# A trunk layer's mixers traced in lanes: visits left out behind reciprocal roots, SSD's time steps in a lane of their own, output projection units taken ahead

## The chip, the core and the metric

The kernel runs on one core of a Trainium2 chip: TensorE (PE) for matmuls, VectorE (DVE), ScalarE (ACT) and GpSimd (POOL) beside it, and SyncE (SP) issuing the transfers. Each engine takes its own instructions in the order in which the program holds them and waits on semaphores for the others. The metric is the device time of one execution in microseconds.

## What is computed

One inference step of a two-layer trunk over 128 context tokens and 256 latent tokens (384 rows of width 1024), in float32. Each layer has a token mixer and a squared-ReLU MLP, both between RMS norms with modulation. The mixer projects the rows once, feeds four scan groups of width 256 (RWKV-7, HGRN2, Mamba-2 SSD, RG-LRU, each forward and backward), concatenates them and projects back:

```python
p = modulated(rms_norm(x, g_pre1), shift, scale) @ w_in
out = concat(rwkv7_mix(...), hgrn2_mix(...), ssd_mix(...), rglru_mix(...))   # each forward + backward
x = x + gate * rms_norm(out @ w_out, g_post1)
# inside ssd_mix, for each direction:
dt = softplus(dtr + dt_bias);  acum = cumsum(dt * a_neg)      # the time steps, 4 heads a direction
# inside rwkv7_mix, after both directions:
y = (y - mean) * rsqrt(var + eps) * ln_w + ln_b               # per head, then bonus and gate
```

## The kernel before

Weights are split into two float32r halves (`unit`: one transfer of 512 KB, a copy on ACT, a difference on DVE), and a projection of 384 rows is 24 matmuls into a `pj` bank. 29 column tiles of `w_in` are projected (`projections`, `ORDER`), each copied to a `st` buffer of the stash; at most seven wait there.

The mixers of a layer are written as Python generators, *lanes*, and `mixers` interleaves them while it traces the program. One pass of its `while` loop is a *round*. In a round every lane gets at most one *visit*: it runs up to its next `yield`. A lane that yielded 0 is visited in the first turn of the next round, one that yielded 1 in the second; one that yielded a condition is visited once the condition holds. After the visits the round is filled with projection steps of four matmuls (`supply`) until some 3 us of estimated TensorE time (`ROUND`) have gone by since its start; where no side lane was seen, six steps are put in in any case. The matmuls are held in exactly this order on PE (`T.ordered`). A program that orders instructions by their data places the other engines' work and the transfers.

The lanes: `t0` to `t3` (`rwkv_thread`) run RWKV's twelve chunk groups (pair, direction, group), each a chain of some 18 visits of small matmuls; `rwkv` prepares their inputs (`rwkv_inputs`, `rwkv_vectors`) and finishes pair 0 as a whole and pair 1 group by group (`rwkv_output`); `hg0` and `hg1` are HGRN2's pairs; `right` joins them (`hgrn_end`) and then does `ssd`; `lru` starts when the last projection is made and has fourteen visits, of which the third to the sixth issue its matmuls. When `hg0`, `hg1`, `right` and `lru` are all done, the lane `tail` is added behind the others: the output projection, one unit of `w_out` after the other, 18 matmuls a unit (three visits), from then on three visits a round. HGRN2's units come first, then SSD's and LRU's, then RWKV's first; RWKV's second comes last, 128 rows at a time.

Four places compute 1/sqrt by `rsqrt` (L284 to L303), a row of twelve or so small DVE operations, and use it on PE one visit later: `channel_rms` (HGRN2's and SSD's norms), `rwkv_inputs` (L1300), `rwkv_output` (L1333, then `flips`, a transposition on PE by matmuls). `ssd` begins with the time steps: a transposition of the `lora` tile, a softplus of some twenty small DVE operations (L716 to L729), the products `dta` (L919, L921), and three sums over tokens on PE in the next visit. All of this lies behind `hgrn_end` in the lane `right`.

Of the kernel before, what the change touches and what calls it, by code (L numbers as in the profile page):

```python
# [20 lines left out]
NCTX, NLAT, NT = 128, 256, 384  # L21
# [10 lines left out]
RIGHT = ("hgrn", "ssd", "lru")  # L32
# [34 lines left out]
NTILE = len(COLS)  # L67
GROUPS = ("rwkv", "hgrn", "ssd", "lru")
# [176 lines left out]
class Trunk:  # L245
# [437 lines left out]
    def layer(self, l, h):  # L683
        a = self.a
        self.l = l
        self.lora = None
        pool = lambda nm, side="left": self.tc.tile_pool(name=f"{nm}{l}", bufs=1, side=side, reuse_waits="tile")
        with pool("mo") as self.mo:
            h = self.mixers(l, h)
        with pool("ff") as fp, pool("kf", "right") as kf, ExitStack() as more:  # L690
            mf, half = more.enter_context(pool("mf", "right")), more.enter_context(ExitStack())
            beside = self.modulations(BESIDE[l], half.enter_context(pool("mg", "right")), 8)
            sums = (step for k, v in SUMS[l] for step in self.modulation_sums(k, v, self.mods[k], mf))
            tags = ("r0", "r1"), ("r2", "h"), ("h", "md")
            finish = self.mlp(l, h, fp, HELD, kf, tags, beside, half, sums)
            then = None
            if l + 1 < L:
                self.prepare(a["win"][l + 1, n] for n in ORDER[:FRESH])
                self.l, n = l + 1, self.mods[l + 1]
                then = n["sh1"], n["sc1"]  # L700
            with self.residual(self.mods[l]["g2"], then, range(3), bufs=2) as (step, h):
                for t in range(3):
                    step(t, finish(t), tags[t])
        return h
# [178 lines left out]
    def channel_rms(self, vs, sqt):  # L883

        T = self.T
        sqs = [self.mt([128, NT], sqt[hf]) for hf in range(2)]
        for hf in range(2):
            self.S.activation(sqs[hf], vs[hf], AF.Square)
        yield 1
        ss = self.bank()  # L890
        for i in range(3):
            for hf in range(2):
                T.matmul(ss[:, i:i + 1], sqs[hf][:, i * 128:i * 128 + 128], self.onec, start=hf == 0, stop=hf == 1)
        m = self.small(3, "crm")
        self.V.tensor_scalar(m, ss[:, 0:3], 1.0 / 256, EPS, op0=OP.mult, op1=OP.add)
        r = self.rsqrt(m, 3, "cr")
        yield 1
        bc = self.bank()
        for i in range(3):
            T.transpose(bc[:, i * 128:i * 128 + 128], r[:, i:i + 1].to_broadcast([128, 128]), self.c("ident"))  # L900
        return bc


    def ssd(self, l):
        V, S, T = self.V, self.S, self.T
        lt = yield from self.lora_tile()
        s0 = self.state("s_ss", [2, 256])
        yield 1
        tp = self.bank()
        for i in range(3):  # L910
# [9 lines left out]
                     self.aneg[l][:, None, 0:4].to_broadcast([128, 3, 4]))  # L920
        V.tensor_mul(an.rearrange("p (i d h) -> p d i h", i=3, d=2)[:, 1], dt[:, 1],  # L921
                     self.aneg[l][:, None, 4:8].to_broadcast([128, 3, 4]))
        yield 1
        cps = self.bank()
        T.matmul(cps[:, 0:12], self.c("le"), a3[:, :, 0:4], start=True, stop=True)
        T.matmul(cps[:, 12:24], self.c("ge"), a3[:, :, 4:8], start=True, stop=True)
# [12 lines left out]
            V.tensor_mul(w4[:, d], w4[:, d], dt[:, d])  # L939
        S.activation(ea, ac, AF.Exp)  # L940
        S.activation(et, et, AF.Exp)

        xbc = []
        for n in range(6):
            acc = self.mt([128, GAP], f"sx{n}")
# [326 lines left out]
    def rwkv_inputs(self, p):  # L1272
# [25 lines left out]
        r = self.rsqrt(m, 6, "rk")  # L1298
        rx = self.mt([128, NT], "rb", 3).rearrange("p (h e) -> p h e", h=6)
        V.tensor_copy(rx, r[:, :, None].to_broadcast([128, 6, 64]))  # L1300
        yield 1
        ps = self.bank()
        for i in range(3):
            T.transpose(ps[:, i * 128:i * 128 + 128], rx[:, 2 * i:2 * i + 2, :].rearrange("p h e -> p (h e)"), ident)
# [13 lines left out]
    def rwkv_output(self, p, lora, bonus, ytok, out, g=None):  # L1318
# [12 lines left out]
        V.tensor_scalar(vr, vr, 1.0 / 64, GN_EPS, op0=OP.mult, op1=OP.add)  # L1331
        r = self.rsqrt(vr, n, "rk")
        V.tensor_mul(y, y, r[:, :, None].to_broadcast([128, n, 64]))  # L1333
        yield 0
        ps = self.bank()
        for i in range(n):
            self.flips(ps[:, i * 64:i * 64 + 64], y[:, i, :])
# [183 lines left out]
    def mixers(self, l, h):  # L1521
# [2 lines left out]

        self.outs, self.made, self.turns, self.taken = {}, {}, [], set()
        self.scans, self.scanned, self.left = {}, set(), {}
        self.groups = [(p, d, g) for p in range(2) for d in range(2) for g in ((0, 2, 1) if d else (0, 1, 2))]
# [8 lines left out]
        with pool("st", "left") as self.stash, pool("rwkv", "left") as rwkv, ExitStack() as early:  # L1538
# [3 lines left out]

            flow = {"proj": self.projections(l, h), "mods": self.modulations(EARLY[l], self.ahead, FRESH)}
            lanes = {"t0": self.rwkv_thread(0), "t1": self.rwkv_thread(1), "t2": self.rwkv_thread(2), "t3": self.rwkv_thread(3),
                     "rwkv": self.rwkv(l),
                     "hg0": self.hgrn(l, 0), "hg1": self.hgrn(l, 1), "right": right(), "lru": self.lru(l)}
            self.lanes, side = lanes, {"hg0", "hg1", "right", "lru"}
            room, kind, waits = dict.fromkeys(lanes, rwkv), dict.fromkeys(lanes, 0), {}
# [28 lines left out]
                self.moded = self.moded or f == "mods" and n < most  # L1577
                return n
            supply("proj", self.T.ns + 1e9, FIRST * 24 // PSTEP)
            n, tail, made = 0, None, 0  # L1580
            while lanes:
                n += 1
                begin = self.T.ns
# [9 lines left out]
                if tail is None:  # L1593
                    if n * MODS > made and not self.moded:
                        made += supply("mods", 1e18, 1)
                    got = supply("proj", begin + ROUND)
                    if not side & seen:
                        got += supply("proj", begin + 1e9, URGENT // PSTEP - got)
                    assert seen or got, (l, n, list(lanes))
                else:  # L1600
                    while "tail" in lanes and (self.T.ns < begin + ROUND or len(lanes) == 1) and visit("tail"):
                        pass
        return self.normed

    def tail(self, l):

# [5 lines left out]
        def split(v, n):  # L1612
# [3 lines left out]
            self.S.activation(hi, v, AF.Copy)  # L1616
            self.V.tensor_sub(lo, v, hi.bitcast(F32))
            return hi, lo
        for i, k in enumerate([2 * GROUPS.index(k) + j for k in RIGHT for j in range(2)] + [0]):
            if k == 0:  # L1620
                yield from self.need("p0")
            w = self.unit(a["wout"][l, k])
            x = split(self.outs[GROUPS[k // 2]][:, k % 2, :], NT)
            for t in tiles:
                self.tokens_by_cols(acc[t], w, x, t, i == 0, False)
                yield 1
        self.prepare(a["w1"][l, n] for n in range(FRESH))

# [33 lines left out]
```

## Time and profile before

| | |
|---|---|
| median of 3 runs | 1466.03 us (1465.28 to 1476.91) |
| the profiled execution | 1468.26 us, span 1466.5 us |
| mean granted TensorE clock | 0.94 |
| mixers, layer 0 and layer 1 | about 98 to 440 us and 765 to 1157 us |
| MLPs, layer 0 and layer 1 | the stretches behind them, to 764 us and to the end |
| HBM traffic over the span | 127 GB/s |

The page gives the busy time of each engine over the span; the waits say which instruction an engine stood still for, and whose result it was; the timeline gives instructions in order of time, with the idle time ahead of one in brackets; the windows give the same busy times for stretches. A granted clock of 1.00 is 2.4 GHz, 0.50 is 1.2 GHz; a mean between them is a mixture.

### The profile page before, as it was taken

How to read it: one execution, taken by the hardware profiler on the slowest of the kernel's cores; microseconds unless marked ns; L12 is line 12 of the kernel's file. 1: busy time of each engine (PE TensorE's matmuls, PEld its weight loads, DVE VectorE, ACT ScalarE, POOL GpSimd, SP SyncE). 2: the span in 40 equal slices, each digit the busy share in tenths (PEclk: the TensorE clock that was granted, in tenths of full speed). 3: DMA queues.
4: the chain of work that ended last, by engine and by line, in shares of the span. 5: the costliest groups of instructions: out<-in, count | busy, mean ns of one | idle time of the engine just before them, and what ended most of it. 6: DMA issues, size and time to landing. Idle time of an engine off the chain costs nothing.

```text
span 1466.5 us, 29196 instructions
## 1 busy us (share of the span) xinstructions
PE 1310.9 (89%) x12128; PEld 1134.5 (77%) x12128; DVE 920.4 (63%) x2155; ACT 578.8 (39%) x1028; POOL 49.9 (3%) x100
## 2 busy tenths in 40 slices
PE   6899997997587989999989999798965789999997
PEld 2678886886366788899869899687854679889986
DVE  4587467956747878395374767766675585424534
ACT  4453224432724332244254533443245434324423
POOL 0002020000001000000010012000000000000000
PEclk9899997998788999999999999999985999999999
DMA  9544331111256867463451111111120463433333
GB/s 336 169 151 149 114 99 55 59 60 55 87 187 197 297 217 234 143 224 131 154 196 62 59 44 56 61 48 47 46 103 10 153 202 118 160 130 129 124 128 122
DMA packets 56321, 187.59 MB, mean 128 GB/s; under 512 B 6492, under 2 KB 9580, under 8 KB 55164
## 3 DMA queue, kind: packets, MB, share of 16 engines
q1 hardware_dynamic: 56188, 185.73, 37.8%
q8 instruction: 95, 1.56, 0.5%
q14 instruction: 38, 0.31, 0.1%
HBM read 178.28 MB, written 7.43 MB: 127 GB/s over the span
## 4 chain that ended last, share of the span: by engine, by line
PE 66%; DVE 19%; DMA 7%; ACT 5%; issue 2%; SPq 0%; POOL 0%; DVEq 0%; ACTq 0%
PE pj L239 31%; PE r L239 17%; PE h L239 12%; PE md L239 5%; DVE wl L614 3%; DMA w<-in_mod_w_dram 2%; DVE ma L492 2%; ACT wh L613 2%; DMA ms<-in_mod_w_dram 2%; DMA gp<-in_norm_g_dram 1%; DMA raw<-in_wout_dram 1%; ACT junk L535 1%; DVE sx L782 1%; DVE rP L1407 1%; DVE x L604 1%
## 5 line engine op out<-in xcount | busy, mean ns | idle before, releaser
L614 DVE TENSOR_TENSOR wl<-raw,wh 128x1024 fp32r<-128x1024 f32 x202 | 247.3, 1224 | 264.9 <-ACT wh L613 262.2
L613 ACT ACTIVATE wh<-raw 128x1024 fp32r<-128x1024 f32 x202 | 213.9, 1059 | 383.2 <-PE md L239 154.6
L239 PE MATMUL pj<-hhi,wl 128*128 128x384 f32 (+2 forms) x1024 | 350.2, 342 | 8.0 <-DVE wl L614 8.0
L239 PE MATMUL pj<-hlo,wh 128*128 128x384 f32 (+2 forms) x1024 | 349.4, 341 | 5.1 <-DVE hlo L567 4.6
L239 PE MATMUL pj<-hhi,wh 128*128 128x384 f32 (+2 forms) x1024 | 351.0, 343 | 2.2 <-ACT relu L626 2.0
L239 PEld LDWEIGHTS pj<-hhi,wh 128*128 128x128 f32 x1024 | 198.8, 194 | 16.3 <-issue 8.2
L239 PEld LDWEIGHTS pj<-hlo,wh 128*128 128x128 f32 x1024 | 198.8, 194 | 12.9 <-issue 5.4
L239 PEld LDWEIGHTS pj<-hhi,wl 128*128 128x128 f32 x1024 | 199.0, 194 | 12.6 <-DVE wl L614 9.6
L492 DVE SCALAR_TENSOR_TENSOR ma<-ms,csil,ma 128x1024 f32<-128x1024 f32 x70 | 86.9, 1277 | 4.0 <-DMA ms<-in_mod_w_dram 4.0
L627 DVE TENSOR_TENSOR relu<-relu 128x384 f32<-128x384 f32 x64 | 35.2, 551 | 1.0 <-ACT relu L626 1.0
L626 ACT ACTIVATE relu<-pj 128x384 f32<-128x384 f32 x64 | 30.3, 474 | 13.2 <-PE pj L239 13.2
L239 PE MATMUL pj<-w,csil 128*32 128x512 f32 x64 | 21.5, 725 | 12.5 <-DMA w<-in_mod_w_dram 12.5
L239 PE MATMUL r<-rI,rW 64*64 64x64 f32 x528 | 31.9, 222 | 0.0
L1434 DVE TENSOR_TENSOR rI<-rI,r 128x256 f32<-128x256 f32 (+1 forms) x66 | 25.0, 392 | 9.9 <-PE r L239 9.3
L1129 ACT ACTIVATE hk<-hK 128x384 f32<-128x384 f32 x24 | 13.5, 564 | 42.3 <-PE r L239 28.4
L239 PE MATMUL r<-rI,rP 64*64 64x64 f32 x480 | 23.4, 223 | 6.8 <-DVE rI L1416 5.1
L239 PEld LDWEIGHTS r<-rI,rW 64*64 64x64 f32 x528 | 24.9, 134 | 5.0 <-issue 3.4
L579 POOL TENSOR_TENSOR xs<-x,scale 128x512 f32<-128x512 f32 x9 | 12.6, 1397 | 469.0 <-DVE x L604 253.6
L239 PEld LDWEIGHTS r<-rI,rP 64*64 64x64 f32 x480 | 18.2, 134 | 12.9 <-issue 5.3
L239 PE MATMUL r<-rW,rI 64*64 64x64 f32 x432 | 27.0, 218 | 0.0
L239 PE MATMUL pj<-wh,o 128*128 128x512 f32 x64 | 22.8, 441 | 3.5 <-ACT wh L613 3.5
L1434 DVE TENSOR_TENSOR rI<-rI,h 128x256 f32<-128x256 f32 (+1 forms) x45 | 17.0, 383 | 12.5 <-PE h L239 11.9
(951 smaller groups left out, 2619.7 us busy)
## 6 DMA issues: line engine op xcount, KB each, us to landing
raw<-in_w_dram SPq DMA_DIRECT2D x128, 512.0 KB
raw<-in_win_dram SPq DMA_DIRECT2D x58, 512.0 KB
mw<-in_mod_w_dram SPq DMA_DIRECT2D x40, 512.0 KB
ms<-in_mod_w_dram SPq DMA_DIRECT2D x40, 512.0 KB
w<-in_mod_w_dram SPq DMA_DIRECT2D x16, 512.0 KB
raw<-in_wout_dram SPq DMA_DIRECT2D x16, 512.0 KB
xd<-x SPq DMA_DIRECT2D x9, 512.0 KB
x<-xd SPq DMA_DIRECT2D x9, 512.0 KB
```

The source lines that it names most:

```text
L239: return self.put(self.engine.matmul(out, left, right, **k), left, right)
L492: V.scalar_tensor_tensor(acc[:, r, :], w, c, acc[:, r, :], op0=OP.mult, op1=OP.add)
L535: self.S.activation(junk, v, AF.Square, scale=1.0 / 32, accum_out=acc[:, i:i + 1])
L604: self.V.scalar_tensor_tensor(v, ys[n], r, v, op0=OP.mult, op1=OP.add)
L613: self.S.activation(hi, v, AF.Copy)
L614: self.V.tensor_sub(lo, v, hi.bitcast(F32))
L626: self.S.activation(r, ps[:, :NT], AF.Relu)
L627: self.V.tensor_mul(r, r, r)
L782: self.V.scalar_tensor_tensor(out, x[:, j:j + GAP], w[j], out, op0=OP.mult, op1=OP.add)
L1129: S.activation(k.rearrange("p (b i t) -> p b i t", i=2, t=h), sides(K, h), AF.Copy)
L1407: V.tensor_mul(prod.rearrange("p u j i t -> p (u j) (i t)"), ps.rearrange("p (q m) -> p q m", q=4), mask[:, None, :].to_broadcast([128, 4, ...
L1434: V.tensor_sub(flat[:, f], flat[:, f], ps[:, 128 if h == 32 else 0:256].rearrange("p (q s) -> p q s", s=64))
```

## The change

The diff is shown but for its empty lines and unchanged neighbours. `rest(n, kind)` yields n + 1 times, so a lane issues nothing for n visits. It stands for one visit in `channel_rms` and in `rwkv_inputs` ahead of the transpositions, and for two visits in `rwkv_output` ahead of the flips. SSD's time steps become a lane `steps` that starts when the `lora` tile is there, in the first round of the mixers, with two visits left out between `dta` and the sums; `ssd` waits for their results. In the first round after the last projection that projects nothing, the first two units of the output projection are requested. In `tail`, the inputs of two units are split ahead of the first unit, and then one unit ahead.

```diff
 # channel_rms, behind r = self.rsqrt(m, 3, "cr")
-        yield 1
+        yield from self.rest(1, 1)
+    def rest(self, n, kind):
+        for _ in range(n + 1):
+            yield kind
-    def ssd(self, l):
+    def ssd_steps(self, l):
         V, S, T = self.V, self.S, self.T
-        lt = yield from self.lora_tile()
-        s0 = self.state("s_ss", [2, 256])
+        yield lambda: self.lora is not None
+        lt = self.lora
         yield 1
         tp = self.bank()
         ...
 # behind the two products into an
-        yield 1
+        yield from self.rest(2, 1)
         cps = self.bank()
         ...
         S.activation(et, et, AF.Exp)
+        self.decays = dt, ac4, w4, ea4, et4
+        yield 1
+    def ssd(self, l):
+        V, S, T = self.V, self.S, self.T
+        s0 = self.state("s_ss", [2, 256])
+        yield lambda: self.decays is not None
+        dt, ac4, w4, ea4, et4 = self.decays
         xbc = []
 # rwkv_inputs, behind V.tensor_copy(rx, ...)
-        yield 1
+        yield from self.rest(1, 1)
 # rwkv_output, behind V.tensor_mul(y, y, r...)
-        yield 0
+        yield from self.rest(2, 0)
 # mixers
-                     "rwkv": self.rwkv(l),
+                     "rwkv": self.rwkv(l), "steps": self.ssd_steps(l),
                     got = supply("proj", begin + ROUND)
+                    if self.first is None and len(self.turns) == NTILE and not got:
+                        self.first = [self.unit(a["wout"][l, k]) for k in self.outward()[:2]]
+    def outward(self):
+        return [2 * GROUPS.index(k) + j for k in RIGHT for j in range(2)] + [0]
 # tail
-        for i, k in enumerate([2 * GROUPS.index(k) + j for k in RIGHT for j in range(2)] + [0]):
+        units, xs = self.first or [], []
+        for i, k in enumerate(self.outward()):
+            while len(xs) <= min(i + 1, 5):
+                xs.append(split(self.outs[GROUPS[self.outward()[len(xs)] // 2]][:, len(xs) % 2, :], NT))
             if k == 0:
                 yield from self.need("p0")
-            w = self.unit(a["wout"][l, k])
-            x = split(self.outs[GROUPS[k // 2]][:, k % 2, :], NT)
+                xs.append(split(self.outs["rwkv"][:, 0, :], NT))
+            w = units.pop(0) if units else self.unit(a["wout"][l, k])
             for t in tiles:
-                self.tokens_by_cols(acc[t], w, x, t, i == 0, False)
+                self.tokens_by_cols(acc[t], w, xs[i], t, i == 0, False)
                 yield 1
```

## Rows read from the trace of the kernel before

**Rows 1.** The page: busy us, share of the span, instructions.

```profile
PE 1310.9 (89%) x12128; PEld 1134.5 (77%) x12128; DVE 920.4 (63%) x2155; ACT 578.8 (39%) x1028; POOL 49.9 (3%) x100
```

**Rows 2.** Waits of PE, whole span: who waited for whom, us in total, times, longest.

```profile
PE h L239 <- DVE ryt L1333: 21.2, 3, 12.1
PE r L239 <- DVE ryt L1333: 20.4, 5, 8.0
...
PE r L239 <- DVE dta L921: 6.2, 1, 6.2
PE h L239 <- DVE dta L921: 5.2, 1, 5.2
...
PE r L242 <- DVE rb L1300: 3.4, 3, 1.5
...
PE h L242 <- DVE crt L301: 2.1, 1, 2.1
```

**Rows 3.** Timeline of PE: start, us, instructions, idle before and its end.

```profile
342.75 0.69 PE L239 MATMUL r<-cst,ryt 64*64 64x64 f32 x8 [3.59 <-DVE ryt L1333]
...
353.88 0.34 PE L239 MATMUL pj<-hhi,wl 128*128 128x384 f32 x1
...
393.00 0.69 PE L239 MATMUL h<-cst,ryt 64*64 64x64 f32 x8 [5.50 <-DVE ryt L1333]
...
407.13 0.69 PE L239 MATMUL r<-cst,ryt 64*64 64x64 f32 x8 [7.98 <-DVE ryt L1333]
407.76 1.22 PE L239 MATMUL pj<-wh,o 128*128 128x512 f32 x2
...
999.81 0.92 PE L239 MATMUL h<-cst,ryt 64*64 64x64 f32 x24 [3.66 <-DVE ryt L1333]
...
1072.63 0.45 PE L239 MATMUL r<-cst,ryt 64*64 64x64 f32 x8 [3.85 <-DVE ryt L1333]
...
1100.74 0.69 PE L239 MATMUL r<-cst,ryt 64*64 64x64 f32 x8 [3.60 <-DVE ryt L1333]
...
1123.58 0.69 PE L239 MATMUL h<-cst,ryt 64*64 64x64 f32 x8 [12.06 <-DVE ryt L1333]
...
1124.92 1.22 PE L239 MATMUL pj<-wh,o 128*128 128x512 f32 x2
...
1131.99 0.63 PE L239 MATMUL pj<-wh,o 128*128 128x512 f32 x2
```

**Rows 4.** Windows: length, busy us by engine, granted clock, DMA share, GB/s.

```profile
50.00:100.00 50.00, 46.66 (x357) 41.01 (x358) 33.71 (x102) 26.57 (x40) 0.61 (x1) 0.91 0.46 153
...
354.00:387.00 33.00, 23.61 (x201) 17.89 (x199) 22.53 (x75) 22.00 (x37) 0.21 (x1) 0.90 0.24 92
387.00:399.00 12.00, 4.82 (x58) 3.88 (x58) 11.41 (x37) 8.43 (x17) 0.00 (x0) 0.64 0.14 57
...
1111.00:1125.00 14.00, 1.94 (x21) 1.41 (x18) 13.51 (x42) 7.18 (x10) 0.00 (x0) 0.50 0.01 1
```

**Rows 5.** The chain that ended last: start, us, what ran there.

```profile
954.58 2.73 PE pj L239 x8
...
965.34 1.61 PE pj L239 x8
```

**Rows 6.** Timeline of DVE: operands of matmuls that stand behind a flip.

```profile
341.46 0.35 DVE L1021 SCALAR_TENSOR_TENSOR sex<-sex,dtq,scm 128x128 f32<-128x128 f32 x1
...
359.44 1.22 DVE L614 TENSOR_TENSOR wl<-raw,wh 128x1024 fp32r<-128x1024 f32 x1
...
361.97 0.55 DVE L1617 TENSOR_TENSOR o<-o_hg,o 128x384 fp32r<-128x384 f32 x1
...
1069.89 0.42 DVE L1045 TENSOR_TENSOR sy<-sy,syo 128x256 f32<-128x256 f32 x1
...
1125.41 0.96 DVE L853 SCALAR_TENSOR_TENSOR o_lr<-o_lr,hhi 128x256 f32<-128x256 f32 x3
```

**Rows 7.** One line's instructions: duration in ns, minimum, median, maximum.

```profile
L921 DVE TENSOR_TENSOR dta<-dtq,aneg x2: 158/162/165, 237.9 to 952.9; 128x12 f32<-128x12 f32 x2
```

More of the change, by code (lines that the diff above doesn't have):

```diff
@@ L685, in layer @@
         self.l = l
-        self.lora = None
+        self.lora = self.decays = None
         pool = lambda nm, side="left": self.tc.tile_pool(name=f"{nm}{l}", bufs=1, side=side, reuse_waits="tile")
@@ L1521, in mixers @@
     def mixers(self, l, h):
+        a = self.a
         self.outs, self.made, self.turns, self.taken = {}, {}, [], set()
@@ L1579, in mixers @@
             supply("proj", self.T.ns + 1e9, FIRST * 24 // PSTEP)
-            n, tail, made = 0, None, 0
+            n, tail, made, self.first = 0, None, 0, None
             while lanes:
```

## The prediction

> **What bounds the kernel now.** I read the page first: PE is busy 1310.9 us of 1466.5, 89%, DVE 63%, ACT 39% [rows 1]. So PE sets the pace nearly everywhere, and what can be won without taking matmuls away is the time in which PE stands still. The waits of PE come next [rows 2]. The reader is to see there that four of the longest are the four chains that the diff touches: the flips of `rwkv_output` behind `ryt` (21.2 + 20.4 = 41.6 us in eight waits), the sums of SSD behind `dta` (6.2 + 5.2 = 11.4 us), the transpositions behind `rb` (3.4 us) and behind `crt` (2.1 us). Together that is 58.5 us, 4% of the span. Third, the timeline of PE says where each wait stands and what is behind it [rows 3]; fourth, the windows say whether DVE or ACT would stop PE next [rows 4].
>
> Two kinds of stretch matter. Up to the last projection (353.9 us in layer 0) the matmul behind a stopped one is mostly a projection with its operands ready: there a removed wait is won whole. Between the last projection and the first matmul of the output projection (407.8 us) lie 53.9 us without such filling [rows 3]; `lru` needs 14 visits there, so a round takes about 3.85 us, and from 387 to 399 us DVE is busy 11.41 of 12 us [rows 4]: there a removed wait may only change its name.
>
> **The change part by part.** The time is summed against the profiled execution, 1468.3 us, which is 2.3 us (0.15%) above the median; I make no difference between them.
>
> *1. SSD's time steps early.* They move from behind `hgrn_end` to the first rounds, nine matmuls and some 22 DVE operations of about 0.16 us [rows 7], 3.5 us a layer; no transfer moves with them but `s0`'s issue, which stays with `ssd`. Two visits are left out between the softplus and the sums; a round is at least some 3 us of matmuls, so three rounds cover a chain whose visible part was 5.2 and 6.2 us [rows 2]. Cover for the DVE work: it is busy 33.7 of 50 us there [rows 4]. Won: 11.4 us. The clock adds something: right behind the wait of layer 1 eight projection matmuls took 2.73 us, later eight take 1.61 [rows 5], 1.1 us, for two layers 2.2. Term: 13.6 us; bounds 5 (the chain collides with RWKV's first inputs, 3.5 us a layer) and 14.
>
> *2. One visit left out in `channel_rms` and `rwkv_inputs`.* The waits are 2.1 and 3.4 us [rows 2], with projections behind them; the extra round is longer than either. Term 5.5; bounds 0 and 5.5. Behind the instruction wait only the lane's own next steps, one round later.
>
> *3. `rwkv_output`, pair 0.* Of the eight waits seven stand in the rows or below; these two are 3.7 us in layer 1 [rows 3] and the remainder, 1.3 us, in layer 0. Projections stand behind both. Term 5.0; bounds 3 and 7.
>
> *4. Pair 1, first group.* 3.6 us at 342.7 and 3.85 at 1072.6 [rows 3]. What comes next on PE is SSD's own: in layer 0 a matmul on `sex`, written until 341.8, in layer 1 a transposition of `sy`, written until 1070.3 [rows 6]. So PE would stand until then under the new name, and 0.9 + 2.3 = 3.2 us are won. Bounds 0 and 7.4.
>
> *5. Pair 1, second group.* 5.5 us at 393.0 and 3.6 at 1100.7, 9.1 us [rows 3]. Behind them stand the last RWKV group and LRU's gates, but the stretch is full on DVE (11.41 of 12 us) [rows 4], and the last group's steps pass through DVE. I take 5, a little over half; bounds 0 and 9.1.
>
> *6. Pair 1, last group.* 8.0 us at 407.1 and 12.1 at 1123.6, both just ahead of the output projection [rows 3]. Here the place in the order decides. In layer 0, by the visits in the code, the flips are in the round in which `tail` starts; two visits later they are behind two rounds of it. The first unit and the first rows for it have been split since 362.5 us [rows 6], so PE goes on at 399.2: 8.0 us. That is also why the units requested ahead are worth nothing: they are there 45 us early already; their two transfers on SP ask for nothing new, and I cost them at nothing. In layer 1 the flips come three rounds ahead of `tail`, and two visits are one too few. But `rwkv_inputs` puts RWKV's second half one round later, and the steps' matmuls and the scans' postponed ones leave more of each round to the projections, so LRU, and with it `tail`, starts about one round sooner. I put the flips one or two rounds behind the start of `tail`. PE would then start it at 1111.5; a first unit there takes 7.1 us (1124.9 to 1132.0, at 1.2 GHz for the most part) [rows 3], and the flips are ready not much before 1122: 9 us won of 12.1. LRU's rows, split from 1126.4 on [rows 6], are needed after four units, which at 7.1 and three times 3.5 us is 1129: no wait. Terms 8 + 9; bounds 4 to 8 and 0 to 12.1.
>
> *The left-out visits themselves* are filled with projections, or with `tail`; the end of the mixers hangs on the last projection, `lru`'s fourteen visits and the units of `tail`, none of which gets longer. If a round is not filled it costs 3.85 us.
>
> The sum: 13.6 + 5.5 + 5.0 + 3.2 + 5 + 17 = 49.3 us. In part 4 over half of a wait came back under another name; the new order on PE will bring more matmuls close to their DVE operands in the stretches behind the last projections, and I take off 5 us for that. 44 us: **1424 us**.
>
> The clock, weighed once more. From 387 to 399 us PE works 4.8 of 12 us at a granted 0.64, and from 1111 to 1125 at 0.50 [rows 4], so the output projection starts at the lower level whether the flips are ahead of it or not; I took nothing back there. The Trainium skill, TensorE: Matmul & The Clock Gate, section HAM oscillation, has it that idle gaps between bursts bring the array down to half its clock, and that the next burst pays; by that rule the denser work of parts 3 to 5 would get some microseconds back that my sum leaves out, and the sparse stretch ahead of `tail` would keep its penalty. The rows above agree with both halves.
>
> **The rivals.** *A. DVE takes over.* Behind the last projection nothing is won: parts 4, 5 and layer 1 of part 6 only rename the wait (`sex`, `sy`, LRU's `hhi`). For it: DVE is busy 11.41 of 12 and 13.51 of 14 us at the two ends [rows 4]. Against it: the output projection's operands are there. Left: 13.6 + 5.5 + 5 + 8 less 5 = 27, so 1441; if the steps also collide, 1450.
>
> *B. Everything is won.* Parts 4 to 6 in full, 7.4 + 9.1 + 20.1, with 24.1 of the others: 61 us, 1407; with clock given back, 1400. Against it: `sex` and `sy` are late by themselves.
>
> *C. It does not do what it says.* The flips stay ahead of `tail` in both layers, and the early waits come back at the next small chain: within 15 us of before, 1455 to 1466. Against it: what stands behind `dta` is a projection.
>
> *D. Slower.* The place is the stretch behind the last projection. The left-out visits let the projections run out sooner while the scans end one to two rounds later, so the stretch grows by up to four rounds a layer at 3.85 us: 8 x 3.85 = 31 us for both. It decides once these rounds are empty rather than filled, and outweighs the rest only if less than half of the early waits (24 us) is won as well: 1468 + 31 - 12 = 1487. Against it: `lru` has its fourteen visits there anyhow, and the postponed scan steps share them.
>
> *E. The clock gives nothing.* The 2.2 us of part 1 stay away, 1426: inside the forecast.
>
> **How the numbers follow.** The forecast, 1410 to 1438, gets 0.55 (E is in it); A 0.20, of which three quarters lie below 1451; B 0.13; C 0.07; D 0.05. From the low ends of the bounds (5 + 0 + 3 + 0 + 0 + 4 = 12 us) time would be 1456, from the high ends 1406. The range that leaves out two in ten is 1402 to 1455. About 1%, 14.7 us, is what a measurement of this kernel tells from no change; so faster 0.55 + 0.15 + 0.13 = 0.83, slower 0.05, and 0.12 within.
>
> **What would show it.** In the waits of PE after: no `dta`; `ryt` below 10 us of 41.6; `rb` and `crt` below 2 together; `sex` and `sy` longer than before. On PE's timeline, flips between matmuls `pj<-wh,o` at the end of both mixers. Layer 0's output projection should start some 20 us sooner, layer 1's some 40 us. The forecast is wrong if `ryt` keeps its two long waits, if DVE results named above take 30 us or more of PE's waits, or if the stretch between last projection and output projection is longer than 54 us.

## The result, and the profile after

| | before | after |
|---|---|---|
| median, measured together | 1465.65 us | 1421.93 us (1418.94 to 1427.14, 4 runs) |
| ratio to before | | 0.9695 (95% interval 0.963 to 0.976) |
| the profiled execution | 1468.26 us, span 1466.5 | 1427.14 us, span 1425.4 |

A second measurement of the changed kernel gave 1420.44 us and a ratio of 0.9685 (0.965 to 0.972); differences below are against this one. Its profiled execution (1419.67 us, span 1417.9) is called the second execution. The forecast was 1424 us, faster. The time is right; the way to it only in part: more than was forecast came ahead of the last projections, and less than half of what was forecast behind them.

The page of the changed kernel, busy time by engine, as [rows 1]:

```profile
PE 1301.6 (91%) x12128; PEld 1126.6 (79%) x12128; DVE 917.5 (64%) x2155; ACT 578.0 (41%) x1026; POOL 50.1 (4%) x100
```

PE's busy time fell by 9.3 us although it does the same 12128 matmuls. The rest of the 41.1 us by which the span is shorter is idle time. Waits of PE after, as [rows 2] (who waited for whom, us in total, times, longest):

```profile
PE pj L239 <- ACT wh L613: 12.8, 3, 7.2
PE h L239 <- DVE ryt L1346: 11.9, 1, 11.9
PE r L239 <- DVE sex L1034: 8.0, 5, 2.7
PE r L239 <- DVE ryt L1346: 5.5, 2, 3.9
PE h L242 <- DVE cry L302: 2.2, 1, 2.2
```

The waits for `dta` and for `rb` ahead of the transpositions in `rwkv_inputs` are gone, and of 41.6 us for `ryt` 17.4 are left, in three waits. One of these is as long as the longest before. The wait for `crt` has only changed its name: at the same transposition PE now stands 2.2 us for `cry`, the last result of the same chain. New at the top is `wh`, the rounded half of a weight, 12.8 us; before it stood at 3.5. PE's timeline shows where each is (start, us, instructions, idle before and its end):

```profile
382.29 0.69 PE L239 MATMUL r<-cst,ryt 64*64 64x64 f32 x8 [3.93 <-DVE ryt L1346]
385.32 1.22 PE L239 MATMUL pj<-wh,o 128*128 128x512 f32 x2
395.91 0.45 PE L239 MATMUL r<-cst,ryt 64*64 64x64 f32 x8
...
423.06 1.22 PE L239 MATMUL pj<-wh,o 128*128 128x512 f32 x2 [5.02 <-ACT wh L613]
...
805.85 0.69 PE L239 MATMUL pj<-hhi,wh 128*128 128x384 f32 x1 [7.16 <-ACT wh L613]
...
1064.38 0.45 PE L239 MATMUL r<-cst,ryt 64*64 64x64 f32 x8 [1.52 <-DVE ryt L1346]
1080.60 0.69 PE L239 MATMUL h<-cst,ryt 64*64 64x64 f32 x8 [11.94 <-DVE ryt L1346]
1081.22 1.22 PE L239 MATMUL pj<-wh,o 128*128 128x512 f32 x2
```

In layer 0 the last group's flips (395.91) stand inside the output projection, which starts at 385.3 instead of 407.8 [rows 3], and PE does not wait for them. In layer 1 they still stand just ahead of it and cost 11.94 us, as before. The output projection there starts at 1081.2 instead of 1124.9 all the same, 43.7 us sooner, of which 17.6 come from layer 0 and its MLP (the first matmul of the norm ahead of layer 1's mixers is at 732.3 instead of 749.9), and 26.1 from layer 1 itself.

The windows split that into work and standing still. A layer's mixers, from the first projection (layer 0) or the norm ahead of them (layer 1) to the output projection, are cut in two at the last projection, as in the prediction. (The table of times ahead of the prediction lets them begin at some 98 and 765 us; the projections and the norm begin sooner.) Columns are the length, busy us of PE, PEld, DVE, ACT and POOL, granted clock, DMA share, GB/s. Before:

```profile
42.40:353.90 311.50, 284.74 (x4089) 250.10 (x4088) 213.06 (x624) 120.97 (x241) 17.93 (x40) 0.94 0.31 101
353.90:407.80 53.90, 29.35 (x268) 22.35 (x266) 41.65 (x141) 33.33 (x56) 0.21 (x1) 0.77 0.24 89
749.90:1076.20 326.30, 295.67 (x4158) 267.57 (x4158) 229.27 (x669) 131.66 (x264) 22.59 (x44) 0.94 0.19 62
1076.20:1124.90 48.70, 25.85 (x197) 18.32 (x195) 33.04 (x111) 32.11 (x54) 0.00 (x0) 0.68 0.21 77
```

and after:

```profile
42.20:336.20 294.00, 277.68 (x4078) 243.57 (x4078) 210.25 (x609) 123.59 (x241) 18.19 (x40) 0.97 0.34 108
336.20:385.30 49.10, 31.65 (x269) 24.26 (x267) 39.55 (x133) 34.03 (x56) 0.20 (x1) 0.77 0.20 76
732.30:1035.70 303.40, 283.62 (x4141) 256.53 (x4142) 226.21 (x664) 131.10 (x262) 22.50 (x44) 0.98 0.20 67
1035.70:1081.20 45.50, 25.73 (x211) 18.53 (x210) 33.97 (x116) 26.36 (x50) 0.00 (x0) 0.69 0.22 82
```

Layer 0's mixers are 22.3 us shorter (365.4 to 343.1), 4.8 of it PE's busy time and 17.5 idle time. Layer 1's are 26.1 us shorter (375.0 to 348.9), 12.2 of it busy time (321.5 to 309.4 for 4353 and 4351 matmuls) and 13.9 idle time (53.5 to 39.6). The second execution tells which of this holds. In each cell the first number is from the rows above, the second from the second execution:

| us less than before | length | idle time of PE | busy time of PE |
|---|---|---|---|
| up to the last projections, both layers | 40.4; 39.9 | 21.3; 21.2 | 19.1; 18.7 |
| from there to the output projection, both layers | 8.0; 4.6 | 10.2; 10.6 | -2.2; -6.0 |
| outside the mixers | -7.3; 4.1 | 0.3; 2.4 | -7.6; 1.7 |

What was gained ahead of the last projections is the same in both, and about half of it is busy time. Behind them idle time fell too, and busy time for the same work rose. What lies outside the mixers differs between two executions of one kernel by 11 us, so it says nothing on the change. Busy time is the clock: by the traces' records of the granted clock PE was busy 123.8 us at 1.2 GHz before, 106.5 and 91.2 after; with that time counted half, PE's busy time over the span is 1249.0, 1248.4 and 1250.9 us.

### The profile page after: what moved, and what is told of

Read it like the earlier page. It is cut to its first block, busy times and chain, and to the rows that moved or that the text cites. A ratio compares the mean times of both kernels' runs of the same rounds, so it can differ in the third digit from the quotient of the medians.

```text
span 1425.4 us, 29177 instructions
## 1 busy us (share of the span) xinstructions
PE 1301.6 (91%) x12128; PEld 1126.6 (79%) x12128; DVE 917.5 (64%) x2155; ACT 578.0 (41%) x1026; POOL 50.1 (4%) x100
## 4 chain that ended last, share of the span: by engine, by line
PE 69%; DVE 16%; DMA 7%; ACT 5%; issue 2%; SPq 1%; POOLq 0%; POOL 0%; DVEq 0%; ACTq 0%
PE pj L239 31%; PE r L239 18%; PE h L239 13%; PE md L239 6%; DVE wl L614 2%; DVE ma L492 2%; DMA ms<-in_mod_w_dram 2%; DMA gp<-in_norm_g_dram 1%; ACT wh L613 1%; DMA w<-in_mod_w_dram 1%; DMA raw<-in_w_dram 1%; ACT junk L535 1%; DMA raw<-in_win_dram 1%; DVE rP L1420 1%; DVE sx L782 1%
## 5 line engine op out<-in xcount | busy, mean ns | idle before, releaser
L627 DVE TENSOR_TENSOR relu<-relu 128x384 f32<-128x384 f32 x64 | 35.2, 550 | 0.7 <-ACT relu L626 0.7
L1447 DVE TENSOR_TENSOR rI<-rI,r 128x256 f32<-128x256 f32 (+1 forms) x58 | 22.0, 392 | 16.6 <-PE r L239 16.0
L1142 ACT ACTIVATE hk<-hK 128x384 f32<-128x384 f32 x24 | 13.5, 564 | 45.9 <-PE h L239 26.1
L239 PE MATMUL r<-rI,rP 64*64 64x64 f32 x568 | 26.5, 221 | 5.3 <-DVE rI L1429 4.2
L239 PEld LDWEIGHTS r<-rI,rP 64*64 64x64 f32 x568 | 21.1, 134 | 10.7 <-ACT rT L1427 3.5
L239 PE MATMUL r<-rI,rW 64*64 64x64 f32 x464 | 28.7, 223 | 0.0
L239 PE MATMUL pj<-wh,o 128*128 128x512 f32 x64 | 23.4, 451 | 5.7 <-ACT wh L613 5.7
L239 PE MATMUL h<-rI,rW 64*64 64x64 f32 x384 | 23.8, 224 | 0.0
L239 PE MATMUL r<-rW,rI 64*64 64x64 f32 x376 | 23.6, 218 | 0.0
```

What stands on the lines that cost most here:

```text
L239: return self.put(self.engine.matmul(out, left, right, **k), left, right)
L627: self.V.tensor_mul(r, r, r)
L1142: S.activation(k.rearrange("p (b i t) -> p b i t", i=2, t=h), sides(K, h), AF.Copy)
L1447: V.tensor_sub(flat[:, f], flat[:, f], ps[:, 128 if h == 32 else 0:256].rearrange("p (q s) -> p q s", s=64))
```

## The experiments

Twelve kernels were measured, each against the kernel before, whose median moved between 1463.3 and 1466.3 us; so ratios are compared. A difference to the changed kernel is that of the two ratios times 1464 us, with the two half intervals put together as the root of the sum of their squares.

| kernel | median, us | ratio to before | against the changed kernel |
|---|---|---|---|
| changed kernel, again | 1420.44 | 0.9685 (0.965 to 0.972) | |
| part 1 taken back | 1425.93 | 0.9730 (0.970 to 0.976) | +6.6 ± 6.4 |
| parts 3 to 6 taken back | 1443.87 | 0.9854 (0.983 to 0.988) | +24.7 ± 6.4 |
| part 2 taken back | 1439.18 | 0.9819 (0.979 to 0.985) | +19.6 ± 6.4 |
| units in turn | 1426.00 | 0.9721 (0.969 to 0.975) | +5 ± 7 |
| part 1 alone | 1459.97 | 0.9956 (0.993 to 0.998) | |
| part 2 alone | 1452.75 | 0.9907 (0.987 to 0.994) | |
| part 2 alone, `rwkv_inputs` only | 1453.44 | 0.9929 (0.990 to 0.996) | |
| two more visits left out | 1413.65 | 0.9644 (0.961 to 0.968) | -6 ± 7 |
| last unit requested first | 1428.11 | 0.9741 (0.971 to 0.978) | +8 ± 7 |
| steps behind the vectors | 1413.35 | 0.9645 (0.961 to 0.968) | -6 ± 7 |
| these two: later steps, two more visits | 1407.28 | 0.9586 (0.955 to 0.962) | -14.5 ± 7.1 |

**The changed kernel again.**

> The changed kernel once more, beside the three that each take one part of it back, so that all four are measured against the kernel before in the same rounds. First measurement: ratio 0.9695 (0.963 to 0.976). The prediction's sum says 1424 us, a ratio of 0.970; a ratio above 0.976 would say that the first measurement was lucky.

The gain is confirmed, with half the uncertainty.

**Part 1 taken back**, SSD's time steps behind HGRN2's end again:

```diff
-    def ssd_steps(self, l):
+    def ssd(self, l):
...
-        yield from self.rest(2, 1)
+        yield 1
...
-                     "rwkv": self.rwkv(l), "steps": self.ssd_steps(l),
+                     "rwkv": self.rwkv(l),
```

> SSD's time steps go back behind HGRN2's end, with no visit left out ahead of the sums; all else stays as in the changed kernel. Theory 1, the prediction's part 1 as it stands: the two waits for `dta` (6.2 and 5.2 us before) come back and cost 11 to 14 us, so about 1435. Theory 2: moving the steps early brought a cost of its own, since their three Exps stand among RWKV's sigmoids on ScalarE at the start of layer 1's mixers, where a split of a weight now comes 7.2 us late: with the steps back that wait goes, and the net is only 4 to 7 us, about 1428. Both expect the `dta` waits in the trace; only theory 2 expects the 7.2 us wait for `wh` near 806 us to be gone.

5.5 us by the medians, 6.6 ± 6.4 by the ratios: the size of theory 2, though the interval reaches the 11 us of theory 1. Its signs are there: the `dta` waits come back with 8.0 and 5.1 us, and no wait for `wh` is left in layer 1's mixers. But the time is not made of them alone. Against the second execution layer 1's mixers are 13.7 us shorter (336.0), layer 0's 0.7 longer, and the output projections are some 10 and 5 us longer. In layer 0 the last group's flips, inside the output projection as before, now wait 6.50 us there. In layer 1 they stand inside it too, with a wait of 3.59 us:

```profile
1079.71 1.22 PE L239 MATMUL pj<-wh,o 128*128 128x512 f32 x2
...
1093.62 0.65 PE L239 MATMUL r<-cst,ryt 64*64 64x64 f32 x8 [3.59 <-DVE ryt L1338]
```

The same two left-out visits put these flips inside the output projection here and just ahead of it in the changed kernel: it is the early time steps that shifted them there.

ScalarE of the changed kernel shows what the wait for `wh` was (start, us, line, operation):

```profile
792.59 0.58 ACT L1363 ACTIVATE rb<-md,par 128x384 f32<-128x384 f32 x1 [2.89 <-PE r L239]
793.19 1.28 ACT L946 ACT_TABLE_LOAD   x1
794.48 0.22 ACT L946 ACTIVATE dea<-dac 128x24 f32<-128x24 f32 x1
...
794.95 1.28 ACT L1364 ACT_TABLE_LOAD   x1
796.25 0.58 ACT L1364 ACTIVATE ra<-r,par 128x384 f32<-128x384 f32 x1
...
804.38 0.47 ACT L430 ACTIVATE st<-pj 128x384 f32<-128x384 f32 x1
804.75 1.04 ACT L613 ACTIVATE wh<-raw 128x1024 fp32r<-128x1024 f32 x1
```

From 792.6 to 804.8 us ScalarE did not pause, and PE's next projection hung on the copy behind all this. The steps' Exp (L946) falls between two sigmoids of RWKV (L1363, L1364), so the table is changed to and back: two of the five loads in that stretch. The Exps and these two loads take 3.1 of the 12.2 us (793.19 to 796.25); the rest is ScalarE's other work. Without the steps there, three such loads lie between 808 and 816 us of the kernel before, and no projection waited.

**Parts 3 to 6 taken back**, no visit left out ahead of the flips in `rwkv_output`:

```diff
-        yield from self.rest(2, 0)
+        yield 0
```

> The visits left out in rwkv_output are taken back, parts 3 to 6 of the prediction; all else stays. Theory 1, the prediction's terms: 5.0 + 3.2 + 5 + 17 = 30 us less up to 5 for collisions, so 25 to 30 us slower than the changed kernel, about 1449; the wait for `ryt` back to some 40 us from 17.4. Theory 2: since layer 1's last flips kept a wait of 11.9 us in the changed kernel, part 6 gave nothing there, and the gain in layer 1 comes from elsewhere (the early steps and projections that run out later): 15 to 20 us slower, about 1440.

23.4 us by the medians, 24.7 ± 6.4 by the ratios: between the two theories, and the interval reaches both. The wait for `ryt` is 41.6 us again, 24.2 more than with the change. That this is also the size of the time is in part luck. Against the second execution the mixers are 23.0 us longer, of which 16.5 are idle time and 6.5 busy time of PE; so idle time grew by two thirds of the 24.2 us, and PE's lower clock added most of the rest. 18.1 of the 23.0 us lie up to the last projections and 4.9 behind them.

**Part 2 taken back**, one visit instead of two ahead of the transpositions in `channel_rms` and `rwkv_inputs`:

```diff
-        yield from self.rest(1, 1)
+        yield 1
```

> The one visit left out in channel_rms and in rwkv_inputs is taken back, part 2; all else stays. Theory 1, the prediction's term: waits for `rb` (3.4 us before) and `crt` (2.1) come back in full, 5.5 us slower than the changed kernel, about 1427.5. Theory 2: the place of these waits is filled or renamed anyway, or the round that it delays costs as much as it saves: within 2 us of the changed kernel.

18.7 us by the medians, 19.6 ± 6.4 by the ratios, more than three times the term: neither theory. The waits are not those of before: PE stands for `cry`, the last result of `rsqrt` in `channel_rms`, 5.87, 5.19 and 4.28 us, where the kernel before stood 2.08, 0.85 and 0.67 us at the same three places. VectorE shows how for the second of them. Here is the chain of layer 0's SSD norm in the kernel before:

```profile
381.15 0.16 DVE L895 TENSOR_SCALAR crm<-r 128x3 f32<-128x3 f32 x1 [1.69 <-PE r L239]
381.34 0.17 DVE L293 TENSOR_SCALAR crb<-crm 128x3 int32<-128x3 int32 x1
...
383.32 0.16 DVE L302 SCALAR_TENSOR_TENSOR cry<-crt,cry 128x3 f32<-128x3 f32 x1
```

and with part 2 taken back:

```profile
389.60 0.16 DVE L895 TENSOR_SCALAR crm<-r 128x3 f32<-128x3 f32 x1 [1.81 <-PE r L239]
389.68 0.42 DVE L837 TENSOR_TENSOR_SCAN hlo<-hlo 128x128 f32<-128x128 f32 x1
390.01 0.14 DVE L293 TENSOR_SCALAR crb<-crm 128x3 int32<-128x3 int32 x1
...
391.95 0.14 DVE L301 TENSOR_TENSOR crt<-crt,crm 128x3 f32<-128x3 f32 x1
392.00 0.15 DVE L839 COPY lu<-hlo 128x1 f32<-128x1 f32 x1
392.07 0.95 DVE L845 TENSOR_TENSOR lu<-lu,o_lr 128x768 f32<-128x768 f32 x1
392.93 0.16 DVE L302 SCALAR_TENSOR_TENSOR cry<-crt,cry 128x3 f32<-128x3 f32 x1
393.00 0.96 DVE L849 TENSOR_TENSOR hhi<-hhi,hlo 128x772 f32<-128x772 f32 x1
...
394.86 0.16 DVE L302 SCALAR_TENSOR_TENSOR cry<-crt,cry 128x3 f32<-128x3 f32 x1
```

The same thirteen operations take 2.33 us when they stand together and 5.42 us when LRU's scans and products of 0.4 to 0.96 us stand between them. How long PE waits for such a chain depends on what the order puts beside it.

**Part 2 alone**, in the kernel before, first at both places and then in `rwkv_inputs` only:

```diff
-        yield 1
+        yield from self.rest(1, 1)
```

> The kernel before with one edit: one visit left out in channel_rms and in rwkv_inputs (part 2 alone). Taking this part back from the changed kernel had cost 18.7 us, where the prediction put 5.5. Theory 1: in the order of before the term was right, 5 to 7 us (the waits for `crt`, `cry` and `rb`, 8.2 us in all, less what is renamed), about 1458; it grew only because the other parts put more VectorE work and less TensorE work between the same instructions. Theory 2: the left-out visit is worth far more in itself, since RWKV's second half starts a round later: 12 us or more, 1452 or less. Rival: nothing, 1464, the waits renamed.

> The kernel before with one visit left out in rwkv_inputs only, and none in channel_rms. With both places it had been 11.7 us faster. Theory 1: the waits decide: this place has the `rb` waits of 3.4 us, so 2 to 4 us, about 1461. Theory 2: the later start of RWKV's second half moves the whole order of layer 1's mixers, and the gain comes from there, with a higher granted clock (TensorE was busy 8.6 us less in that layer with both places): 8 to 12 us, about 1454, and again some 8 us less busy time there.

11.7 us (by the ratio 13.6 ± 5.0), and 9.9 us (10.4 ± 4.2) for `rwkv_inputs` alone: theory 2 in both, though at the edge of its bound in the first. The listed waits do not explain it: with `rwkv_inputs` alone PE still stands 9.6 us for `dta`, and 43.4 for `ryt` and 10.4 for `cry`, more than before. Layer 1's mixers do, here with both places (first row) and `rwkv_inputs` only (second):

```profile
751.70:1112.20 360.50, 312.92 (x4352) 278.63 (x4352) 260.83 (x782) 162.49 (x316) 22.54 (x44) 0.92 0.20 66
```

```profile
748.40:1113.20 364.80, 314.76 (x4352) 281.27 (x4352) 262.23 (x782) 165.23 (x318) 22.52 (x44) 0.92 0.19 66
```

Against the 375.0 us and 321.5 busy us of before, 8.6 of 14.5 and 6.8 of 10.2 us are busy time of PE for the same matmuls, the rest is idle time. Layer 0 is 1 to 3 us shorter. So with RWKV's second half a round later PE stands still less in layer 1, and there the larger part of the gain is the clock. That is read from one execution each; the two of the changed kernel differ by 0.2 us of busy time in layer 1's mixers, by 4.1 in layer 0's.

**Part 1 alone**, in the kernel before:

```diff
-    def ssd(self, l):
+    def ssd_steps(self, l):
...
+                     "rwkv": self.rwkv(l), "steps": self.ssd_steps(l),
```

> The kernel before with SSD's time steps early and two visits left out ahead of their sums (part 1 alone). Theory 1, the prediction's term: 13.6 us, about 1450.5. Theory 2: the steps' three Exps cost up to 7.2 us on ScalarE at the start of layer 1's mixers, in this order as well, and what is left is 5 to 8 us, about 1457.5. Theory 3, from taking part 2 alone, where 11.7 us came out of waits of 5.5 us and TensorE was busy 8.6 us less in layer 1 for the same matmuls: the clock in layer 1's mixers comes back, and the gain is above 16 us, below 1448.

6.4 ± 3.5 us: the size of theory 2, and not its reason. No wait for `wh` stands in layer 1's mixers here. What came in its place is on PE's timeline:

```profile
232.40 0.87 PE L242 MATMUL h<-cst,cry 128*128 128x128 f32 x3 [5.86 <-DVE cry L302]
...
812.50 0.55 PE L242 MATMUL h<-cst,rb 128*128 128x128 f32 x3 [2.38 <-DVE rb L1314]
...
936.37 0.55 PE L242 MATMUL h<-cst,rb 128*128 128x128 f32 x3 [2.50 <-DVE rb L1314]
```

With a `rb` of 1.45 us in layer 0 and three more `cry` (0.77, 4.28, 1.97) these are 19.2 us, where the kernel before has 7.0 for the same transpositions. 12.2 us came in under the names of part 2 while the 11.4 us of `dta` went out. What was won all the same is in layer 1, whose mixers are 12.8 us shorter, 7.4 of it busy time (314.1 instead of 321.5 us), while layer 0's got 6.4 us longer. So the 7.2 us wait for `wh` is no cost of part 1 by itself; it is in all five kernels that have parts 1 and 2 with the steps in the first round, and in none of the five with one of the two.

**Units in turn**, the first two units and their rows requested when the output projection starts:

```diff
-                    if self.first is None and len(self.turns) == NTILE and not got:
-                        self.first = [self.unit(a["wout"][l, k]) for k in self.outward()[:2]]
...
-            while len(xs) <= min(i + 1, 5):
...
+            w = self.unit(a["wout"][l, k])
+            x = split(self.outs[GROUPS[k // 2]][:, k % 2, :], NT)
```

> The output projection requests its first two units when it starts, and splits the inputs of a unit just ahead of it, as before; all else as in the changed kernel. Theory 1, the prediction: worth nothing, since units and rows had been there 45 us early before the change: within 2 us of the changed kernel (1420), same start of the output projection. Theory 2: since the output projection now starts some 10 us sooner after the last projection, the early request carries its first units: 3 to 8 us slower, with waits for `wh` or `o` at its start.

5 ± 7 us: not told apart from nothing. In the profiled executions the mixers are 1.5 and 1.8 us longer than in the changed kernel's second one, and PE does not wait for `wh` or `o` at the start of either output projection, so theory 2 is not shown, and theory 1 not excluded.

**Two more visits left out** ahead of the flips of pair 1:

```diff
-        yield from self.rest(2, 0)
+        yield from self.rest(2 if g is None else 4, 0)
```

> Four visits instead of two are left out ahead of the flips of pair 1's three groups; all else as in the changed kernel (1420 us in its second measurement). Theory 1, the prediction's part 6, with one visit too few in layer 1: two more put layer 1's last flips behind two units of the output projection; the wait of 11.9 us falls below 3 and the time by 8 to 10 us, to about 1411. Theory 2, as in its rival A: the wait changes its name, to the rows of LRU that the fifth unit needs or to RWKV's last rows at the end; within 3 us of the changed kernel.

6 ± 7 us by the ratios, 6.8 by the medians: neither theory is excluded by the time alone. The wait of 11.9 us is gone; PE's timeline around the start of layer 1's output projection:

```profile
1071.57 0.48 PE L239 MATMUL r<-rw,rI 64*64 64x64 f32 x4 [3.13 <-ACT rw L1465]
...
1074.57 1.22 PE L239 MATMUL pj<-wh,o 128*128 128x512 f32 x2
...
1087.16 0.74 PE L239 MATMUL pj<-wl,o 128*128 128x512 f32 x2 [2.14 <-DVE wl L614]
...
1092.63 0.45 PE L239 MATMUL r<-cst,ryt 64*64 64x64 f32 x8
```

The flips (1092.63) wait for nothing. In their place PE stands 3.13 us for the last chain's own `rw`, and 2.14 us for a unit, which PE now reaches before its second half is made. From the last projection to the output projection layer 1 takes 39.8 instead of 45.7 us, and the output projection itself, up to 1113.2 us in both, 38.6 instead of 35.2 us. Idle time in the first of these stretches is 10.8 us less, busy time 4.9 us more, at a granted clock of 0.63 instead of 0.65. From its norm to the end of its output projection layer 1 takes 387.1 us here and 387.8 in the second execution, so the profiled execution, the slowest of the six, does not show the 6.8 us.

**The output projection's last unit requested ahead of the MLP's first two:**

```diff
-        self.prepare(a["w1"][l, n] for n in range(FRESH))
+        w = self.unit(a["wout"][l, 1])
+        self.prepare(a["w1"][l, n] for n in range(FRESH))
...
-        w = self.unit(a["wout"][l, 1])
```

> The output projection's last unit is requested ahead of the MLP's first two instead of behind them; all else as in the changed kernel. Theory 1: the 5.0 us that PE stands at the end of layer 0's output projection for `wh` come from the order of requests on SyncE's queue, behind two units that nobody needs yet: they go, and the time falls by 4 to 5 us, to about 1415.5. Theory 2: the transfers are the limit in that stretch (288 to 305 GB/s), and the wait moves to the MLP's first units: no difference (within 2 us).

The wait goes, as theory 1 has it, and the time does not fall: 1428.11 us, if anything slower (+8.2 ± 7.1). In the second execution of the changed kernel that wait was 2.18 instead of 5.02 us, so there was less to win than it seemed. What PE no longer waits for here it waits for at the norm behind the output projection (6.32 us for its statistics instead of 4.31). Why the median is some 8 us higher is not settled; in its profile 4.7 us are PE's busy time ahead of layer 1's output projection, at a granted 0.60 instead of 0.65 with the same 212 matmuls.

**Time steps behind RWKV's first vectors:**

```diff
-        yield lambda: self.lora is not None
+        yield lambda: (0, 0) in self.scans and (0, 1) in self.scans
```

> The lane of SSD's time steps starts once RWKV's first pair has its vectors for both directions, instead of in the first round; all else as in the changed kernel. Theory 1: the 7.2 us that PE stands for `wh` near 806 us come from the three Exps between RWKV's sigmoids, with five table loads of 1.28 us in 10 us: the wait falls below 1 us, the `dta` waits stay away, and the time falls by 5 to 7 us, to about 1414. Theory 2: the table loads come with RWKV's own sigmoids and exponentials, and ScalarE is late there without the steps: the wait stays, within 2 us of the changed kernel.

7.1 us by the medians, 6 ± 7 by the ratios. No wait for `wh` stands in layer 1's mixers, and no wait for `dta` came back. The mixers of layer 1 are 341.5 instead of 349.7 us, those of layer 0 344.5 instead of 346.2. Up to the last projection of layer 1 PE stands still 13.7 us instead of 20.1. That is theory 1's size, though the interval alone does not exclude that nothing was won.

**Both together:**

> The changed kernel with both edits that each measured some 7 us below it: the time steps start behind RWKV's first vectors, and two more visits are left out ahead of pair 1's flips. Theory 1, both are gains of their own: 14 us below the changed kernel, 1406. Theory 2, as the segments of the profiled executions had it: the later steps give 7 us and the two more visits at most 3, since the last chain's own waits and a slower first unit take the place of the 11.9 us: 1410 to 1414.

1407.28 us, 14.5 ± 7.1 below the changed kernel and 4.1% below the kernel before. That is the size of theory 1; the interval also reaches the 6 to 10 us of theory 2. The intervals of this ratio and the changed kernel's do not touch. No wait for `ryt`, `dta` or `wh` is left in the mixers:

```profile
41.90:379.90 338.00, 306.95 (x4346) 266.38 (x4346) 246.96 (x736) 148.98 (x289) 18.20 (x41) 0.95 0.32 105
721.20:1057.40 336.20, 313.02 (x4344) 277.55 (x4344) 246.68 (x740) 149.11 (x303) 22.57 (x44) 0.94 0.21 71
```

In layer 1 idle time is 23.2 us, of 39.6 in the changed kernel and 53.5 before.

## Why the prediction was right, and where it was not

**The sum is right and its places are not.** Up to the last projections the prediction had 13.6 + 5.5 + 5.0 + 3.2 = 27.3 us, and 40.4 came (39.9 in the second execution). Behind them it had 5 + 17 less 5 for collisions = 17 us, and 8.0 came (4.6). That the two errors nearly cancel, and that the time is within 4 us of the forecast, is luck.

**The clock is what the first of these lacked:** 2.2 us were put in, from one pair of rows [rows 5], and 19.1 came there (18.7). In the kernel before the clock fell behind the waits. Around the one for `dta` in layer 1, which ended at 953.1 us:

```profile
941.90:953.90 12.00, 5.64 (x83) 5.11 (x81) 10.63 (x38) 8.70 (x13) 0.17 (x3) 0.84 0.26 89
953.90:965.90 12.00, 11.52 (x123) 10.51 (x123) 5.96 (x20) 4.42 (x10) 0.00 (x0) 0.73 0.14 44
965.90:977.90 12.00, 12.00 (x174) 10.80 (x175) 7.92 (x22) 4.40 (x11) 0.16 (x3) 1.00 0.14 47
```

Behind pair 0's `ryt` in layer 1 it was 0.88 from 1001.9 to 1013.9 us, with PE busy throughout. In the changed kernel it is 1.00 from 816.0 us to the last projection at 1035.7. The rule that the prediction cited, the Trainium skill, TensorE: Matmul & The Clock Gate, section HAM oscillation, was borne out in both halves, and the first was worth more than the "some microseconds" that the prediction gave it. The second half is the sparse stretch: its granted clock stayed at 0.77 in layer 0 and 0.68 to 0.69 in layer 1 (0.69 and 0.65 in the second execution).

**Behind the last projections less idle time went than was put in,** 10.2 us (10.6) for the 17, and PE took 2.2 us (6.0) longer over the same work. The waits of parts 5 and 6 mostly went: the second group's fell from 9.1 to 5.45 us (I took 5 as won), and the last group's 8.0 us in layer 0 went, with the flips among the matmuls of the output projection, as said. But the stretch that held layer 0's two got only 4.8 us shorter (1.6). The step that failed is that a wait gone here is time won: part 6 counted it in full, and the 5 us for collisions did not cover what came back.

**Layer 1's half of part 6 failed by its place.** I put the flips one or two rounds behind the start of `tail`; they are in its first round, visited ahead of it, and the wait is 11.94 us of 12.06. With part 1 taken back they stand where I put them, so the early steps, which I had put down as a help, moved them the other way; by which lane, no run shows. Two more visits took the wait away; the gain of 6 ± 7 us is not told apart from nothing. The 40 us by which layer 1's output projection was to start sooner came out (43.7, and 46.9 in the second execution), but with 12.2 of layer 1's own 26.1 us from the clock.

**Part 1 (13.6 us) was too large.** It gave 6.4 alone, and taking it back cost 5.5. The step that failed is "there a removed wait is won whole": the matmul behind `dta` was a projection, as said, but further on in the same round order the transpositions behind `cry` and `rb` waited 12.2 us more. Whether PE came to them sooner or their operands were written later is not shown.

**Part 2 (5.5 us) was too small,** 11.7 alone and 18.7 in the changed kernel. The two waits of [rows 2] were taken as the price of these places. They were the price in that order alone. (Nor were they among the longest waits, as the prediction has it: by total time `rb` is fifteenth and `crt` eighteenth.)

**Parts 1 and 2 together came out:** the kernel with parts 3 to 6 taken back has just these two and the units, 1443.87 us, 20.1 below before, and the two terms are 19.1. Alone they gave 6.4 and 11.7 us, some 18 in all, so in time they add up within the uncertainty, although the waits change names between them.

**Parts 3 to 6 (30.2, less 5 for collisions)** gave 23.4 us by the medians, with 24.2 us less of `ryt`; 16.5 of it were idle time and 6.5 clock. Of the waits ahead of the last projections pair 0's two (5.0) went, as said, and so did the first group's (7.4, I took 3.2) in both layers; `sex` got only 1.2 us longer and `sy` 0.9 shorter.

Of the signs: no `dta`, true; `rb` of `rwkv_inputs` and `crt` gone, true by name, but `cry` has 2.2 us in place of `crt`'s 2.1 (3.4 in the second execution); `ryt` below 10 us, false (17.4); `sex` and `sy` longer, only `sex`; flips inside the output projection, in layer 0 only; output projections some 20 and 40 us sooner, true (22.4 and 43.7); the stretch ahead of it not above 54 us, true (49.1 and 45.5). One sign of being wrong was met as it was written: the waits for the named DVE results, `ryt`, `sex` and `sy`, come to 30.0 us. The bound was badly set, since `sex` and `sy` had 12.3 us before. Of the rivals, B did not come about, and C holds for the one place in layer 1. A was right in part: behind the last projections little was won, 8.0 us (4.6) of 17, and its time of 1441 us was missed since ahead of them the clock gave so much. Rival D's empty rounds did not come: those stretches got shorter by 4.8 and 3.2 us.

Not foreseen at all was ScalarE. I counted the steps' matmuls and VectorE operations and not their three Exps. In the order of the changed kernel PE waits 7.2 us behind them and RWKV's own table loads; with the steps started later that wait is gone.

## What to carry to other kernels

Where an order is fixed on one engine, a wait's row is what it costs in that order; expect the next serial chain of small operations to wait in the place of the one that was freed. Price a removed wait by where it stands. In the dense stretch here the clock gave back about as much as the idle time did, and in the sparse one it took some of the idle time's gain away; read both from the busy time of the same matmuls in whole stretches, not from one pair of rows. Profile the changed kernel twice: what differs between the two is not the change. When work is moved, look at every engine that it touches in its new place, ScalarE's tables among them, and at what it moves further on in the order.

## What the runs showed of the hardware

- Thirteen dependent operations of 0.14 to 0.17 us on a few columns step by 0.2 us when nothing is between them, 2.33 us in all; with other work of VectorE between them 5.42 us.
- The same 4350 matmuls of a layer kept PE busy 321.5 us in one order and 309.4 us in another (309.5 in the second execution), at mean granted clocks of 0.91 and 0.94 (0.93). Over the whole span the busy times of 1310.9, 1301.6 and 1296.5 us become 1249.0, 1248.4 and 1250.9 with the time at 1.2 GHz counted half.
- A change of ScalarE's table is seen as a row of 1.28 us with the next operation 0.01 to 0.02 us behind it (793.19 and 794.48) and the one before it ended 0.02 us ahead. The Trainium skill, ScalarE: Activation LUTs, section What ACT_TABLE_LOAD costs, has the same load at about 1283 ns but about 2.66 us for a switch, with a drain; in this trace no such drain shows.
